# Diagonal weight tiles of a depthwise convolution, built during an earlier layer and kept in DRAM, loaded by DMA where they are used

## The chip, the cores and the metric

One core of a Trainium2 chip runs the whole program. The metric is the device time of one execution in microseconds (us); the median of three runs stands for a kernel.

The engines are named as the profile names them: PE is TensorE (matmuls; PEld are its weight loads), DVE is VectorE, ACT is ScalarE, POOL is GpSimd, and SP is the engine whose queue issues most of the DMAs here.

## The reference

A trunk of four layers on 512 tokens of width 1024. Layer 0 and layer 3 mix tokens by sliding-window attention, layer 1 by a conformer convolution module, layer 2 by a gated linear recurrence; every layer then has an MLP with squared ReLU and an inner width of 4096. All of it is float32. The part that matters here is the convolution module:

```
def conformer_conv(h, w_pw1, b_pw1, w_dw, b_dw, ln_g, ln_b, w_pw2, b_pw2):
    u = h @ w_pw1 + b_pw1
    a, gate = jnp.split(u, 2, axis=-1)
    u = a * jax.nn.sigmoid(gate)
    up = jnp.pad(u, ((0, 0), (CONV_WIDTH - 1, 0), (0, 0)))
    c = lax.conv_general_dilated(up, w_dw[:, None, :].astype(up.dtype), window_strides=(1,), padding='VALID',
                                 dimension_numbers=('NWC', 'WIO', 'NWC'), feature_group_count=D_MODEL)
    c = c + b_dw
    c = jax.nn.silu(layer_norm(c, ln_g, ln_b))
    return c @ w_pw2 + b_pw2

def squared_relu_mlp(h, w1, w2):
    return jnp.square(jax.nn.relu(h @ w1)) @ w2
```

`CONV_WIDTH` is 31, and each of the 1024 channels has its own 31 weights.

## The kernel before

**Matmuls and weights.** Every large matmul is done in float32 by three products of split operands (`step`, lines 285 to 287): high by high, high by low, low by high. A weight piece of 512 KB is loaded by a DMA on SP's queue into a tile `raw` (`fetch`, lines 245 and 251; `get`, line 212, for the MLP's second matrix), ScalarE casts it to `wh`, and VectorE makes `wl` = raw - wh (both line 262). There are three `raw` buffers for the first kind, eight for the second, and five pairs `wh`, `wl`. SP issues in the order in which the DMAs stand in its queue: one that waits for a buffer holds those behind it. GpSimd adds further pieces to a `raw` by accumulating DMAs on its own queue (line 217).

**The MLP** (`mlp`) runs four groups of 1024 inner columns. A group is a `linear` of 64 steps, whose eight PSUM tiles ScalarE squares into `us`, and then seven products of 56 steps in all, a fast 2 by 2 scheme. The products read operands `uh`, `ul` that VectorE and ScalarE make from `us` and its sums (lines 541 to 556), and VectorE adds each product into the rows (line 595).

**The convolution module** (`conformer`) runs a `linear` over eight channel blocks of 128. A block has two PSUM tiles, gate and `a`. `glu` takes each from PSUM on VectorE (line 921), ScalarE makes the sigmoid of the gate (line 924), and VectorE multiplies (line 930). Blocks 0 to 2 are then convolved on VectorE by 30 multiply-adds each over the row (line 884, "taps"). Blocks 3 to 7 are convolved on TensorE (`on_pe`): sixteen small ScalarE copies rearrange the block into `u` (line 903), four groups of nine matmuls each multiply it with a block-diagonal weight tile (line 824; the trace shows each as two), and sixteen small ScalarE copies bring the result out of PSUM (line 910). VectorE adds bias and shift (line 913; line 895 for the blocks of its own taps). Sums of the block and of its square are collected for the layer norm (`sums`, lines 849 to 861), and ones-matmuls turn them into means (`token_means`, line 401). When the last block is done, mean and scale are spread by TensorE (line 391), each block is centred, scaled and activated (lines 955 to 969), and the second projection begins.

**The weight tiles.** `Convolution` keeps them. A tile `w` is 128 x 34 x 32 floats, 557 KB; there are 20, four for each of the five blocks. `prepare` copies the 31 weights of the channels to a zeroed tile `taps` (line 802, sixteen copies of 32 partitions), and `build` multiplies `taps` with a 32 x 32 identity pattern `i4` on VectorE (line 814). Ten are built ahead, into ten buffers; each group used makes room for the next.

**What sets the order.** Work beside the matmuls is written as generators (`spawn`); each matmul step resumes them (`pump`), and `yield n` lets n steps pass. That gives the program's order, and a scheduler then fixes the order of each engine's own instructions. VectorE's taps are spaced by `PACE` steps. Each engine runs its instructions strictly in order.

## Time and profile before

| | us |
|---|---|
| median of three runs (2174.43 to 2178.05) | 2176.84 |
| profiled execution | 2178.24 |
| span of its trace | 2176.2 |
| PE busy | 2126.1 (98%) |
| DVE busy | 1417.7 (65%) |
| ACT busy | 1155.8 (53%) |
| POOL busy | 200.5 (9%) |

The profiled execution is 1.4 us above the median, and its trace covers all but 2.0 us of it. The first MLP lies at about 165 to 500 us of the span, the convolution module at about 500 to 730.

A row of a timeline gives the start and the duration in us, the engine, the line, the operation, its output and inputs, the shapes and how many instructions the row stands for; in brackets how long the engine stood idle before it, and what released it. Busy time of PE hides short waits between its matmuls, because their ends are modelled.

### The profile page before, as it was taken

The numbers are of one execution on the slowest core, as the hardware profiler recorded it, in microseconds if no ns is written. First come the engines' busy times: TensorE is split into PE (matmuls) and PEld (weight loads), VectorE is DVE, ScalarE is ACT, GpSimd is POOL, SyncE is SP. The second block draws the span as 40 slices with busy tenths as digits, with TensorE's granted clock in tenths as the row PEclk, the third lists the DMA queues.
The fourth block names the chain that finished last, engine by engine and source line by source line (L and its number), as shares of the span: only waits on it lengthen the run. The fifth ranks groups of instructions, "written<-read, shape, count | busy, mean of one in ns | idle before, by whom it ended". The sixth has DMA issues, their size and how long they took to land.

```text
span 2176.2 us, 27268 instructions
## 1 busy us (share of the span) xinstructions
PE 2126.1 (98%) x10226; PEld 1745.1 (80%) x10226; DVE 1417.7 (65%) x2250; ACT 1155.8 (53%) x2015; POOL 200.5 (9%) x193
## 2 busy tenths in 40 slices
PE   8999999999988999999999999999999999999997
PEld 7778788888877888888788888887888878888886
DVE  6864664759985375475888874547558784547547
ACT  6855454454684445445555554544546684534545
POOL 0000110110020011011300000101100000101100
PEclk9999999999998999999999999999999999999999
DMA  4154756745214375664322225567564116567553
GB/s 150 49 153 111 182 126 154 184 68 136 69 39 136 97 169 122 166 172 92 89 63 78 78 69 174 116 165 164 119 170 87 61 47 196 114 157 174 120 132 77
DMA packets 211063, 262.56 MB, mean 121 GB/s; under 512 B 9027, under 2 KB 136003, under 8 KB 210932
## 3 DMA queue, kind: packets, MB, share of 16 engines
q1 hardware_dynamic: 175540, 191.61, 27.7%
q0 software_dynamic: 35392, 69.21, 20.2%
q8 instruction: 81, 1.33, 0.3%
q14 instruction: 50, 0.41, 0.1%
HBM read 258.69 MB, written 2.10 MB: 120 GB/s over the span
## 4 chain that ended last, share of the span: by engine, by line
PE 71%; DVE 17%; ACT 4%; DMA 4%; issue 3%; SPq 0%; DVEq 0%; ACTq 0%
PE mm L287 20%; PE mm L286 20%; PE mm L285 20%; DVE wl L262 7%; DMA raw<-in_mlp_w_dram 4%; DVE rows L595 3%; DVE ul L556 2%; PE aux L745 2%; ACT wh L262 1%; PE aux L695 1%; PE aux L1059 1%; PE aux L438 1%; PE aux L824 1%; ACT uc L903 1%; DVE us_sum L547 1%
## 5 line engine op out<-in xcount | busy, mean ns | idle before, releaser
L262 DVE TENSOR_TENSOR wl<-raw,wh 128x1024 fp32r<-128x1024 f32 x452 | 550.9, 1221 | 528.4 <-ACT wh L262 525.1
L262 ACT CAST wh<-raw 128x1024 fp32r<-128x1024 f32 x452 | 467.9, 1047 | 492.5 <-DMA raw<-in_mlp_w_dram 206.1
L285 PE MATMUL mm<-x,wh 128*128 128x512 f32 x1568 | 629.9, 402 | 0.0
L287 PE MATMUL mm<-x,wl 128*128 128x512 f32 x1568 | 614.5, 392 | 7.6 <-DVE wl L262 7.6
L286 PE MATMUL mm<-x,wh 128*128 128x512 f32 x1568 | 613.3, 391 | 0.0
L287 PEld LDWEIGHTS mm<-x,wl 128*128 128x128 f32 x1568 | 294.5, 188 | 73.9 <-DVE wl L262 11.3
L285 PEld LDWEIGHTS mm<-x,wh 128*128 128x128 f32 x1568 | 295.3, 188 | 58.4 <-DVE rows L595 3.7
L286 PEld LDWEIGHTS mm<-x,wh 128*128 128x128 f32 x1568 | 295.3, 188 | 56.7 <-issue 1.8
L217 POOL DMA_DIRECT2D raw<-in_mlp_w_dram x128 | 153.5, 1206 | 1779.7 <-DVE wl L262 974.9
L285 PE MATMUL mm<-wh,uh 128*128 128x512 f32 x768 | 302.5, 394 | 7.1 <-DVE rows L595 4.4
L286 PE MATMUL mm<-wl,uh 128*128 128x512 f32 x768 | 299.2, 390 | 0.0
L287 PE MATMUL mm<-wh,ul 128*128 128x512 f32 x768 | 297.5, 390 | 0.2 <-DVE ul L556 0.2
L285 PEld LDWEIGHTS mm<-wh,uh 128*128 128x128 f32 x768 | 144.1, 188 | 45.7 <-DVE rows L595 8.1
L287 PEld LDWEIGHTS mm<-wh,ul 128*128 128x128 f32 x768 | 144.1, 188 | 31.2 <-DVE ul L556 0.6
L286 PEld LDWEIGHTS mm<-wl,uh 128*128 128x128 f32 x768 | 144.2, 188 | 28.2
L561 ACT ACTIVATE relu<-mm 128x512 f32<-128x512 f32 x128 | 75.9, 593 | 159.1 <-PE mm L287 159.1
L556 DVE TENSOR_TENSOR ul<-us,uh 128x1024 fp32r<-128x1024 f32 x64 | 78.0, 1219 | 32.5 <-ACT uh L555 32.5
L595 DVE SCALAR_TENSOR_TENSOR rows<-mm,nr,rows 128x512 f32<-128x512 f32 x128 | 95.1, 743 | 0.0
L562 ACT ACTIVATE us<-relu 128x512 f32<-128x512 f32 x128 | 81.0, 632 | 4.0
L285 PE MATMUL mm<-wh,y 128*128 128x512 f32 x192 | 78.0, 406 | 1.4 <-ACT y L366 1.4
L426 ACT ACTIVATE sq<-rows 128x512 f32<-128x512 f32 x64 | 40.2, 628 | 68.6 <-DVE rows L338 54.3
L287 PE MATMUL mm<-wh,y 128*128 128x512 f32 x192 | 76.0, 398 | 0.0
(232 smaller groups left out, 2564.8 us busy)
## 6 DMA issues: line engine op xcount, KB each, us to landing
raw<-in_mlp_w_dram SPq DMA_DIRECT2D x256, 512.0 KB
raw<-in_mlp_w_dram POOLq DMA_DIRECT2D x128, 512.0 KB, 6.1
raw<-in_hgrn_w_qfig_dram SPq DMA_DIRECT2D x64, 256.0 KB
raw<-in_attn_w_qkv_dram SPq DMA_DIRECT2D x20, 512.0 KB
raw<-in_attn_w_o_dram SPq DMA_DIRECT2D x16, 512.0 KB
raw<-in_conv_w_pw_dram SPq DMA_DIRECT2D x32, 256.0 KB
raw<-in_conv_w_pw_dram SPq DMA_DIRECT2D x8, 512.0 KB
raw<-in_hgrn_w_o_dram SPq DMA_DIRECT2D x8, 512.0 KB
```

The source lines that it names most:

```text
L217: gp.dma_start(out=wide(to), in_=block(w, r, c, h), accum_op=ALU.add)
L262: return sc.copy(wh, raw), ve.tensor_tensor(wl, raw, wh.bitcast(F32), ALU.subtract)
L285: pe.matmul(ps, sh, mh, start=start, stop=False, skip_group_check=again)
L286: pe.matmul(ps, sh, ml, start=False, stop=False, skip_group_check=again)
L287: pe.matmul(ps, sl, mh, start=False, stop=stop, skip_group_check=again)
L426: sc.activation(scratch("sq"), rows[:, b, f * T : (f + 1) * T], AF.Square, accum_out=self.ms[:, f, b : b + 1])
L438: pe.transpose(ps[:, b * P : (b + 1) * P], rows[:, b, j * P : (j + 1) * P], ident)
L556: ve.tensor_tensor(flat[1], src, flat[0].bitcast(F32), ALU.subtract)
L561: sc.activation(s, ps, AF.Relu)
L562: sc.activation(us[j // KH][:, :, j % KH, :], s.rearrange("p (h t) -> p h t", h=2), AF.Square)
L595: ve.scalar_tensor_tensor(o, banks[bank][p], norm.r2[sign][:, b : b + 1], o, ALU.mult, ALU.add)
L745: pe.matmul(po[h * HD : (h + 1) * HD, n * P : (n + 1) * P], vtok[:, n - 1 + b, kv * HD : (kv + 1) * HD], pT[:, b, n - n0, h, :], start=b = ...
```

## The change

The 20 weight tiles are no longer built in the convolution module. `prepare` takes a pool of the MLP of layer 0 and runs there as a task beside it: 40 half tiles of 128 x 17 x 32 floats are built on VectorE (line 809) in one buffer, and each is stored by a DMA on SP's queue to a tile in DRAM (line 812). In the convolution module `build` loads a whole tile by a DMA on SP's queue (line 832). Three things go with it: `PACE` falls from 2.4 to 1.8 steps per tap; the two accumulators of the layer norm get tiles of their own; and for the last block, 7, every second small copy, before and after its matmuls, goes to VectorE (line 920).

```diff
-PACE = 2.4
+PACE = 1.8
...
+            if beside:
+                spawn(beside(mp))
...
         def __init__(self):
...
+            dram = ctx.enter_context(tc.tile_pool(name="dram", bufs=1, space=bass.MemoryType.DRAM))
+            self.stored = [dram.tile([P, self.TAPS, 32], F32, name=f"w{n}") for n in range(4 * CONV_ON_PE)]
+            self.taps = const.tile([P, CONV_ON_PE, 4, self.TAPS], F32, name="taps")
...
+        def prepare(self, pool):
+
+            yield 24
             j0, r0 = KC - CONV_ON_PE, vrows["w_dw"]
...
+            nx = self.TAPS // 2
+            for n, stored in enumerate(self.stored):
+                for x in (0, nx):
+                    w = pool.tile([P, nx, 32], F32, tag="w", name="w")
+                    taps = self.taps[:, n // 4, n % 4, x : x + nx]
+                    ve.tensor_tensor(
+                        w, self.i4.unsqueeze(1).broadcast_to([P, nx, 32]), taps.unsqueeze(2).broadcast_to([P, nx, 32]), ALU.mult
+                    )
+                    nc.sync.dma_start(out=stored[:, x : x + nx, :], in_=w)
+                    yield 9
...
+        def ahead(self):
             for _ in range(self.AHEAD):
+                yield 4
                 self.build()
-                yield 3
...
-            ve.tensor_tensor(
-                w, self.i4.unsqueeze(1).broadcast_to([P, nx, 32]), self.taps[:, n // 4, n % 4, :].unsqueeze(2).broadcast_to([P, nx, 32]), ALU.mult
-            )
+            w = self.cp.tile([P, self.TAPS, 32], F32, tag="w", name="w", bufs=self.AHEAD)
+            nc.sync.dma_start(out=w, in_=self.stored[n])
...
-                    shared[k] = tmp.tile([P, T], F32, tag="acc", name=k, bufs=2)
+                    shared[k] = cp.tile([P, T], F32, name=k)
...
+            ends = j == KC - 1
+
+            def copy(o, src, r):
+                (ve.tensor_copy if ends and r % 2 else sc.copy)(o, src)
...
-                    sc.copy(cs[j][32 * g : 32 * g + 32, r::4], ps[32 * r : 32 * r + 32, :])
+                    copy(cs[j][32 * g : 32 * g + 32, r::4], ps[32 * r : 32 * r + 32, :], r)
...
-        mlp(i, mid, norm)
+        mlp(i, mid, norm, conv.prepare if i == 0 else None)
```

The order of the instructions moves at three places that matter.

VectorE in the linear of the first MLP's group 1, before, from the last product added into the rows (L595) to the sum of the first halves (L541):

```order
L595 SCALAR_TENSOR_TENSOR rows<-mm,r_1893,rows 128x512
L262 TENSOR_TENSOR wl<-raw,wh 128x1024 x5
L556 TENSOR_TENSOR ul<-us,uh 128x1024
L262 TENSOR_TENSOR wl<-raw,wh 128x1024 x4
L556 TENSOR_TENSOR ul<-us,uh 128x1024
L541 TENSOR_TENSOR us_sum<-us 128x1024
```

and in the change, from the same place on (L597 is the former L595, L558 the former L556):

```order
L597 SCALAR_TENSOR_TENSOR rows<-mm,r_1917,rows 128x512
L262 TENSOR_TENSOR wl<-raw,wh 128x1024
L809 TENSOR_TENSOR w<-i_145,taps 128x544 x2
L262 TENSOR_TENSOR wl<-raw,wh 128x1024
L809 TENSOR_TENSOR w<-i_145,taps 128x544
L262 TENSOR_TENSOR wl<-raw,wh 128x1024
L809 TENSOR_TENSOR w<-i_145,taps 128x544 x2
L262 TENSOR_TENSOR wl<-raw,wh 128x1024
L809 TENSOR_TENSOR w<-i_145,taps 128x544
L262 TENSOR_TENSOR wl<-raw,wh 128x1024
L558 TENSOR_TENSOR ul<-us,uh 128x1024
L809 TENSOR_TENSOR w<-i_145,taps 128x544 x2
```

One or two builds now stand before each cast. Of the 40 builds seven stand in the attention's projection, twelve in group 0's linear, thirteen in group 1's (one of them ahead of the row shown first, four behind the row shown last, before the second ul) and eight in group 2's; none stands among the products.

SP's queue at the same place, before, with the raw loads of the linear (L251) and of the products (L212):

```order
L251 DMA raw<-in_mlp_w_dram 128x4x256 x7
L212 DMA raw<-in_mlp_w_dram 128x2x512 x8
L251 DMA raw<-in_mlp_w_dram 128x4x256 x8
L212 DMA raw<-in_mlp_w_dram 128x2x512 x8
L251 DMA raw<-in_mlp_w_dram 128x4x256 x8
```

and in the change, from the products' loads of group 0 on:

```order
L212 DMA raw<-in_mlp_w_dram 128x2x512 x6
L251 DMA raw<-in_mlp_w_dram 128x4x256 x3
L812 DMA w_133<-w 128x544
L251 DMA raw<-in_mlp_w_dram 128x4x256 x2
L812 DMA w_134<-w 128x544 x2
L251 DMA raw<-in_mlp_w_dram 128x4x256
L812 DMA w_135<-w 128x544
L251 DMA raw<-in_mlp_w_dram 128x4x256
L812 DMA w_135<-w 128x544
L812 DMA w_136<-w 128x544
L251 DMA raw<-in_mlp_w_dram 128x4x256
L812 DMA w_136<-w 128x544
```

The stores (`w_133` and so on are the tiles in DRAM) stand among the raw loads, the first of the group behind three of them.

VectorE at the end of the convolution's linear, before, from the end of block 1's taps:

```order
L884 SCALAR_TENSOR_TENSOR uc<-uc,vecT 128x493
L895 TENSOR_TENSOR uc<-uc,shift 128x512
L913 SCALAR_TENSOR_TENSOR uc<-uc,vecT,shift 128x512
L262 TENSOR_TENSOR wl<-raw,wh 128x1024
L921 TENSOR_TENSOR a<-mm,r_4308 128x512
L884 SCALAR_TENSOR_TENSOR uc<-uc,vecT 128x494
L930 SCALAR_TENSOR_TENSOR a<-a,vecT,gate 128x512
L884 SCALAR_TENSOR_TENSOR uc<-uc,vecT 128x495
```

and in the change (L900, L911, L934, L942 and L951 are the former L884, L895, L913, L921 and L930):

```order
L900 SCALAR_TENSOR_TENSOR uc<-uc,vecT 128x511
L911 TENSOR_TENSOR uc<-uc,shift 128x512
L942 TENSOR_TENSOR a<-mm,r_4474 128x512
L262 TENSOR_TENSOR wl<-raw,wh 128x1024
L934 SCALAR_TENSOR_TENSOR uc<-uc,vecT,shift 128x512
L942 TENSOR_TENSOR a<-mm,r_4474 128x512
L951 SCALAR_TENSOR_TENSOR a<-a,vecT,gate 128x512
L262 TENSOR_TENSOR wl<-raw,wh 128x1024
L920 COPY uc<-a 32x128 x8
L934 SCALAR_TENSOR_TENSOR uc<-uc,vecT,shift 128x512
L875 TENSOR_TENSOR acc_4832<-acc_4832,uc 128x512
L876 TENSOR_TENSOR acc_4833<-acc_4833,csq 128x512
```

All taps, block 2's too, now stand ahead of block 7's two tiles; behind them come VectorE's share of the small copies of block 7 and the sums of block 6.

## Rows read from the trace of the kernel before

**Rows 1.** Page, part 1: engine, busy us (share of the span) x instructions
```profile
PE 2126.1 (98%) x10226; PEld 1745.1 (80%) x10226; DVE 1417.7 (65%) x2250; ACT 1155.8 (53%) x2015; POOL 200.5 (9%) x193
```

**Rows 2.** Windows: us; busy of PE, PEld, DVE, ACT, POOL; granted clock; DMA share; GB/s
```profile
520.00:540.00 20.00, 20.00 (x90) 16.57 (x89) 20.00 (x26) 7.59 (x9) 0.00 (x0) 1.00 0.50 132
560.00:580.00 20.00, 19.25 (x114) 15.65 (x113) 16.25 (x22) 16.63 (x37) 0.00 (x0) 1.00 0.15 53
660.00:665.00 5.00, 4.62 (x22) 4.47 (x21) 0.17 (x1) 0.00 (x0) 0.00 (x0) 0.50 1.04 387
```

**Rows 3.** Timeline of PE after the linear: start us, us, instruction, count [idle before <-releaser]
```profile
622.77 9.48 PE L824 MATMUL aux<-uc,w 128*128 128x128 f32 x72
...
641.26 11.75 PE L824 MATMUL aux<-uc,w 128*128 128x128 f32 x72 [9.01 <-ACT uc L910]
...
657.53 3.55 PE L401 MATMUL aux<-ones_d,acc 128*128 128x1 f32 x16 [4.52 <-ACT csq L854]
...
663.12 1.84 PE L401 MATMUL aux<-ones_d,csq 128*128 128x1 f32 x8
...
670.59 0.80 PE L285 MATMUL mm<-wh,z 128*128 128x512 f32 x1 [1.58 <-ACT z L366]
```

**Rows 4.** Timeline of DVE at the end of the convolution
```profile
627.95 0.75 DVE L913 SCALAR_TENSOR_TENSOR uc<-uc,vecT,shift 128x512 f32<-128x512 f32 x1 [3.40 <-ACT uc L910]
...
629.75 0.68 DVE L921 TENSOR_TENSOR a<-mm,r 128x512 f32<-128x512 f32 x1
...
631.41 1.75 DVE L930 SCALAR_TENSOR_TENSOR a<-a,vecT,gate 128x512 f32<-128x512 f32 x1
...
646.60 8.79 DVE L884 SCALAR_TENSOR_TENSOR uc<-uc,vecT 128x503 f32<-128x503 f32 x9
```

**Rows 5.** Timeline of ACT at the end of the convolution
```profile
611.37 6.96 ACT L903 COPY uc<-a 32x128 f32<-32x128 f32 x16 [4.52 <-DVE a L930]
...
633.19 6.83 ACT L903 COPY uc<-a 32x128 f32<-32x128 f32 x16 [2.49 <-DVE a L930]
...
640.03 5.87 ACT L910 COPY uc<-aux 32x128 f32<-32x128 f32 x15
```

**Rows 6.** The lines L814 and L802: duration ns min/median/max, first and last start
```profile
L814 DVE TENSOR_TENSOR w<-i,taps x20: 1277/1281/1294, 515.9 to 616.2; 128x1088 f32<-128x1088 f32 x20
...
L802 DVE COPY taps<-vecT x16: 236/249/329, 508.0 to 515.6; 32x155 f32<-32x155 f32 x16
```

**Rows 7.** Timeline of DVE in the first MLP, groups 0 and 1
```profile
171.15 1.41 DVE L447 SCALAR_TENSOR_TENSOR x<-aux,vecT,x 128x512 fp32r<-128x512 f32 x2
...
212.93 1.23 DVE L262 TENSOR_TENSOR wl<-raw,wh 128x1024 fp32r<-128x1024 f32 x1 [1.49 <-ACT wh L262]
...
293.74 1.23 DVE L262 TENSOR_TENSOR wl<-raw,wh 128x1024 fp32r<-128x1024 f32 x1 [6.93 <-ACT wh L262]
...
296.46 1.23 DVE L262 TENSOR_TENSOR wl<-raw,wh 128x1024 fp32r<-128x1024 f32 x1 [1.49 <-ACT wh L262]
...
298.71 1.23 DVE L556 TENSOR_TENSOR ul<-us,uh 128x1024 fp32r<-128x1024 f32 x1 [1.02 <-ACT uh L555]
```

**Rows 8.** Timeline of ACT at the start of group 1
```profile
252.78 1.05 ACT L262 CAST wh<-raw 128x1024 fp32r<-128x1024 f32 x1 [6.17 <-DMA raw<-in_mlp_w_dram]
...
262.30 1.05 ACT L262 CAST wh<-raw 128x1024 fp32r<-128x1024 f32 x1 [0.53 <-DMA raw<-in_mlp_w_dram]
```

**Rows 9.** Timeline of SP at the start of group 1
```profile
246.94 3.96 SPq L251 DMA_DIRECT2D raw<-in_mlp_w_dram  x3
```

**Rows 10.** Timeline of SP, the last output store
```profile
2172.69 0.33 SPq L511 DMA_DIRECT2D out_dram<-rows  x1
```

**Rows 11.** Waits of SP: line waited for, us in total, times, longest
```profile
SPq L1261 <- DMA out_dram<-rows: 1.7, 1, 1.7
```

**Rows 12.** Page, part 6: DMA issues, count, KB each, median us to landing
```profile
raw<-in_mlp_w_dram POOLq DMA_DIRECT2D x128, 512.0 KB, 6.1
```

**Rows 13.** Windows, raw loads of the first MLP
```profile
166.00:175.00 9.00, 9.00 (x49) 7.46 (x49) 6.33 (x12) 6.52 (x11) 0.00 (x0) 1.00 0.77 235
```

31 lines of the change are left out of this document (14 added, 17 removed).

## The prediction

> **What bounds the kernel now.** The page's first part comes first: TensorE is busy for 98% of the span [rows 1], so an edit elsewhere pays only where TensorE stands still. The windows by stretch show where that is. In the convolution's linear (520 to 580) TensorE is nearly always busy, 19.25 of 20 us at the worst; behind it, at 660 to 665, it runs at half the granted clock, 0.50 [rows 2]. The timeline of TensorE shows the stretch between [rows 3]: the linear ends at 622.8; block 6's 72 convolution matmuls follow; then TensorE is idle for 9.01 us until ScalarE's PSUM copies (L910) free it, and for 4.52 us before the means (L401); the first projection matmul comes at 670.59, some 48 us after the linear.
>
> Why the two waits are there is read from VectorE and ScalarE. Block 7's last tile is ready at 622.9, but VectorE takes it (L921) at 629.75, because L913 of block 5, which stands before it in VectorE's order, waited 3.40 us for ScalarE's L910; L930 then lasts until 633.16 [rows 4]. ScalarE waits for L930 twice: 4.52 us at block 6 and 2.49 us at block 7. Its sixteen copies of block 7 (0.43 us each) run from 633.19 to 640.03, and the PSUM copies of block 6, which hold the banks block 7 needs, stand behind them [rows 5]. So VectorE, loaded with taps and weight tiles, is the first cause; ScalarE's chain of small copies passes it on; and nine taps left over hold VectorE from 646.60 to 655.39, ahead of block 7's last shift [rows 4].
>
> **The change part by part.**
>
> *Taken out of the convolution's VectorE.* Twenty builds at a pitch of about 1.21 us (1.28 us each, overlapping) are 24.2 us, and sixteen tap copies at 0.26 are 4.2 us [rows 6]: 28 us. The faster pace puts some 20 taps (about 0.66 us each) ahead of the last tile that ran behind it before: 13 us back. VectorE gains about 15 us before 623 and keeps up. Block 6's gated tile, late by at least the 4.52 us that ScalarE waited, moves up, ScalarE's queue with it, and L934 of block 5 (L913 before) no longer holds block 7's last tile.
>
> *The tail, step by step.* Last tile from PSUM at 623.2, gated (0.6 + 0.74) at 624.5. ScalarE, after its casts and squares, starts its eight copies at about 625.6 and ends at 629.0; VectorE's eight, at 0.25 us by the nearest row [rows 6], end sooner. Block 6's PSUM copies follow at 629.0 and free the first bank by 630.6. TensorE ends block 6 at 632.0 and goes on to block 7 there, not at 641.26. Its 72 matmuls take 9.4 us, and about 2 us of waiting for the partial sums (L875, L876), whose means now stand among them: end near 643.5. Four last PSUM copies, ScalarE and VectorE in turn, 1.4 us, shift 0.75, square 0.63: 646.5. Of the 32 ones matmuls 16 are left (1.84 us for eight at half clock [rows 3]): 650. From there as now (664.96 to 670.59, 5.63 us) to the first projection matmul at about 655. Gain 15.5 us: 13 if something slips by a PSUM copy or two, 19 if the clock stays at full speed.
>
> *Less waiting for VectorE in the linear.* The 0.75 us missing at 560 to 580 [rows 2] goes: 0.8 us.
>
> *The loads.* Twenty of 557 KB, 11.1 MB on SP's queue. At the 235 GB/s that loads reach in the first MLP [rows 13] each takes 2.4 us, 47 us in all, in a stretch where the engines are half busy at first and 0.15 later [rows 2]. Tiles lie ten ahead, so I take 0; without that cover the price is what a late raw load costs, up to 2 us.
>
> *The builds in the first MLP.* Forty at half size, 0.64 us each by the row of the full ones: 26 us. All stand in the linear phases or in the attention's projection, where VectorE idles up to 6.93 us at a time [rows 7]; none stands among the products. Their work is covered. What is not is the single buffer: a build waits until the store before it has landed, and the casts queued behind it on VectorE wait too, as do the raw loads behind a store on SP.
>
> *What a store's flight is.* The trace has no such store. The nearest row is the last output store, same queue and direction, twice the size: 0.33 us of issue and a wait of 1.7 us [rows 10, 11] give at least 2.0, and by the span's end at most 3.5. The far end is an accumulating load, 6.1 us [rows 12]. I take 2.6, and 1.1 more (half a raw load of 512 KB at 235 GB/s) when a raw load is just ahead. Spacing of two builds: 0.64 + 2.6 = 3.2 us plain, 4.3 behind a raw load.
>
> *Group 0.* Twelve builds, five of them behind raw loads: 7 x 3.2 + 5 x 4.3 = 44 us, against 41.8 us from the x rows at 171.15 to the cast at 212.93 [rows 7]. Part of the raw loads is ahead by then, and the products' first operands have slack: 1.5 us, with the projection's seven builds. *Group 1* is worse, because it begins in a backlog. Three raw loads are issued from 246.94 [rows 9]; ScalarE gets the first at 252.78 and the third at 262.30 [rows 8], 12 us after issue. The phase's first store stands behind them and cannot land before about 263.5. Eleven spacings of about 3.6 us follow: the last build ends near 304, where now the last cast runs at 296.46 and the operand ul at 298.71 [rows 7]. That operand would be 7 us late; the second product needs it about 1.5 us after it is ready now: TensorE loses about 6 us. *Group 2* has eight builds, which end near 287 by the same count, with time to catch up: 0. Cost 7.5 us. The ends: with landings of 2.0 us group 1's last build ends by 293, cost 0.5; with 6.1 us everywhere, 12 x 6.7 - 42 = 39, 263.5 + 74 - 296 = 41, and some 8, near 90 us. The output store is nearer than an accumulation, so the range takes spacings of up to 4.3 us: 12 x 4.3 - 41.8 = 10 and 263.5 + 11 x 4.3 + 0.6 - 296.5 = 15, 25 us.
>
> By the Trainium skill, DMA: Bandwidth & Descriptors, section "Latency and other measured facts", memory latency is 0.2 us on average but 2 us at high load, and it makes most of a transfer's fixed cost. By that rule a store among raw loads would land some 1.8 us later than one in the quiet end of the kernel, whose row I used; the spacing would be about 5 us, an estimate, the two groups would cost 41 us, and the sum would be 2202 us. No row here shows a store under load.
>
> **The sum.** The profiled execution took 2178.24 us. 2178.24 - 15.5 - 0.8 + 7.5 = 2169.4; it stands 1.4 us above the median of the runs, so 2168 us. A measurement of this kernel can tell about 0.2%, 4.4 us: "same" is 2172.5 to 2181.2.
>
> **The rivals.**
> *The stores pace the first MLP (slower).* One mechanism: VectorE waits for a landing before each build, and the lateness reaches the products' operands. It decides from a mean spacing of about 4.2 us, where groups 0 and 1 cost 9 and 14 us, more than the gain, and the time passes 2181; at 4.5 they cost 12 and 17, and the time is 2178.2 - 16.3 + 29 - 1.4 = 2190. For it: loads in group 1 do take 6 to 12 us [rows 8, 9], and the operand is on the path. Against: only the first store of that phase stands behind three loads, the later ones behind one or none. The page's rule above is this case with a price. Chance 0.16.
> *The tail stays bound by small copies.* ScalarE's PSUM copies and the alternation of two engines on one bank could keep half of the waits, and the edit on VectorE would matter little: gain 8 instead of 15.5, 2175.5. For it: the 9.01 us name ScalarE, not VectorE. Against: ScalarE itself waits for L930 [rows 5]. Chance 0.13.
> *Better than forecast.* Stores land in 2.0 us, cost 0.5, and the clock, which fell after TensorE had stood idle, stays up, gain 19: 2178.2 - 19.8 + 0.5 - 1.4 = 2157.5. Chance 0.16.
> The forecast itself, 2160 to 2175, has 0.55.
>
> **How the numbers follow.** The range takes the best case's 2155 at one end and, at the other, spacings of up to 4.3 us, 2178.2 - 16.3 + 24 - 1.4 = 2184; beyond lies the rest of the slower rival. Faster by over 0.2%: the best case, nine tenths of the forecast and a little of the copies' rival, 0.68; slower 0.16; same 0.16.
>
> **What would show it.** Right: in the changed profile block 7's 72 matmuls start within 1 us of block 6's end; L951 of block 7 ends before 626; the first projection matmul comes about 48 - 15 = 33 us after the linear; in group 1's linear VectorE idles before L809 for landings, ul comes some 7 us later against the phase's start, and group 0 loses under 3 us. Wrong: idle time before L809 adding up to far more than 3 us a build, or TensorE waiting for ul or wl by over 15 us in the first MLP; a wait of over 3 us between blocks 6 and 7; new waits for raw loads in the convolution's linear.

## The result, and the profile after

| | us |
|---|---|
| before, median of six runs on this chip (2174.43 to 2178.28) | 2177.69 |
| changed kernel, median of six runs (2186.02 to 2194.43) | 2190.31 |
| ratio, with its 95% interval | 1.0059 (1.0049 to 1.0070) |
| changed kernel, profiled execution | 2188.81 |
| span of its trace | 2187.1 |

The change makes the kernel slower by 0.6%. The forecast was 2168 us with a range of 2155 to 2184, faster with 0.68: wrong in sign, and 2190 lies outside the range.

Three marks split the time in every trace. **A** is the first transpose of the rows behind the first MLP (L438), **B** the first of block 6's 72 convolution matmuls, where the linear of the convolution module ends, **C** the first projection matmul. Before they stand at 493.75, 622.77 and 670.59 us. The timeline of TensorE in the changed kernel:

```profile
506.98 0.27 PE L438 MATMUL aux<-ident,rows 128*128 128x128 f32 x1
...
578.18 1.81 PE L884 MATMUL aux<-uc,ones 128*128 128x512 f32 x2 [4.52 <-DVE uc L900]
...
641.48 9.48 PE L840 MATMUL aux<-uc,w 128*128 128x128 f32 x72
652.46 5.17 PE L840 MATMUL aux<-uc,w 128*128 128x128 f32 x24 [1.50 <-ACT uc L920]
658.84 1.02 PE L401 MATMUL aux<-ones_d,acc 128*128 128x1 f32 x8 [1.20 <-DVE acc L875]
...
661.30 8.74 PE L840 MATMUL aux<-uc,w 128*128 128x125 f32 x46
672.61 1.02 PE L401 MATMUL aux<-ones_d,uc 128*128 128x1 f32 x8 [2.58 <-DVE uc L934]
...
680.52 0.80 PE L285 MATMUL mm<-wh,z 128*128 128x512 f32 x1 [1.58 <-ACT z L366]
```

A stands 13.2 us later than before: that is the price of what now stands ahead of it, the tap copies, the builds and the stores (e1 below has the copies alone and loses 0.8 us). From A to B the linear takes 134.5 us (129.0 before): it became 5.5 us longer. From B to C it is 39.0 us against 47.8: here are the gains, 8.8 us of the 15.5 forecast. Of the waits of [rows 3] the 9.01 us between blocks 6 and 7 are down to 1.50, and in place of the 4.52 us before the means there are 1.20 before the partial sums and 2.58 before the last means. But a new wait of 4.52 us stands in the middle of the linear, before L884, the ones matmul that takes the shift from block 0; it waits for L900, block 0's last tap on VectorE. Behind that wait the granted clock is 0.50 from 578.43 to 581.84, so the linear loses more than the wait itself. In all 13.2 + 5.5 - 8.8 = 9.9 us at C, and 10.6 at the end of the profiled execution.

The windows of the changed kernel, beside [rows 2] (us; busy of PE, PEld, DVE, ACT, POOL; granted clock; DMA share; GB/s):

```profile
560.00:580.00 20.00, 15.48 (x64) 11.82 (x63) 17.42 (x24) 11.91 (x22) 0.00 (x0) 0.96 0.30 91
620.00:640.00 20.00, 20.00 (x120) 16.90 (x119) 16.99 (x20) 15.89 (x34) 4.63 (x3) 1.00 0.37 133
640.00:660.00 20.00, 17.30 (x114) 14.88 (x113) 12.78 (x17) 17.00 (x41) 6.35 (x4) 0.91 0.17 53
660.00:680.00 20.00, 16.10 (x88) 14.76 (x86) 7.25 (x22) 5.47 (x12) 0.00 (x0) 0.68 0.43 160
```

The hole in the linear is the first row, 15.48 of 20 us. In the last row the granted clock is 0.68 in the mean, so part of it at 1.2 GHz in place of 2.4, over the 46 matmuls of block 7 and the means: TensorE had stood still three times behind B, for 1.50, 1.20 and 2.58 us. The page's first part hardly shows any of it; it stands against [rows 1]:

```profile
PE 2132.3 (97%) x10226; PEld 1746.5 (80%) x10226; DVE 1427.9 (65%) x2286; ACT 1149.4 (53%) x1999; POOL 199.2 (9%) x193
```

VectorE at the end of the convolution, beside [rows 4]:

```profile
576.15 1.23 DVE L262 TENSOR_TENSOR wl<-raw,wh 128x1024 fp32r<-128x1024 f32 x1 [2.35 <-ACT wh L262]
577.29 0.74 DVE L900 SCALAR_TENSOR_TENSOR uc<-uc,vecT 128x511 f32<-128x511 f32 x1
...
626.21 1.75 DVE L951 SCALAR_TENSOR_TENSOR a<-a,vecT,gate 128x512 f32<-128x512 f32 x1
...
643.01 1.23 DVE L262 TENSOR_TENSOR wl<-raw,wh 128x1024 fp32r<-128x1024 f32 x1 [5.67 <-ACT wh L262]
...
645.28 0.68 DVE L942 TENSOR_TENSOR a<-mm,r 128x512 f32<-128x512 f32 x1
646.00 1.33 DVE L951 SCALAR_TENSOR_TENSOR a<-a,vecT,gate 128x512 f32<-128x512 f32 x1
...
649.58 4.27 DVE L920 COPY uc<-a 32x128 f32<-32x128 f32 x8
```

Block 7's tile leaves PSUM (L942) at 645.28 and is gated from 646.00 on, 4.5 us behind B. The wait that was L913's [rows 4] has moved to the cast ahead of it: wl waits 5.67 us for ScalarE's wh, which stands behind ScalarE's copies of block 6. The tap that L884 needs, at 577.29, stands behind such a cast too.

VectorE in the first MLP, beside [rows 7]: first the group of the 40 builds (busy, mean ns of one, idle time before them), then the timeline of group 1.

```profile
L809 DVE TENSOR_TENSOR w<-i,taps 128x544 f32<-128x544 f32 x40 | 29.0, 725 | 71.6 <-DMA w<-w 70.3 <-PE aux L747 1.2
```

```profile
177.29 0.73 DVE L809 TENSOR_TENSOR w<-i,taps 128x544 f32<-128x544 f32 x1 [1.63 <-DMA w<-w]
...
268.63 0.72 DVE L809 TENSOR_TENSOR w<-i,taps 128x544 f32<-128x544 f32 x1 [3.71 <-DMA w<-w]
...
288.05 0.72 DVE L809 TENSOR_TENSOR w<-i,taps 128x544 f32<-128x544 f32 x1 [0.59 <-DMA w<-w]
293.42 0.72 DVE L809 TENSOR_TENSOR w<-i,taps 128x544 f32<-128x544 f32 x1 [4.64 <-DMA w<-w]
294.06 1.22 DVE L262 TENSOR_TENSOR wl<-raw,wh 128x1024 fp32r<-128x1024 f32 x1
296.29 0.72 DVE L809 TENSOR_TENSOR w<-i,taps 128x544 f32<-128x544 f32 x1 [1.01 <-DMA w<-w]
...
302.62 0.72 DVE L809 TENSOR_TENSOR w<-i,taps 128x544 f32<-128x544 f32 x1 [4.47 <-DMA w<-w]
...
310.17 1.22 DVE L558 TENSOR_TENSOR ul<-us,uh 128x1024 fp32r<-128x1024 f32 x1
```

and the matmul that reads the operand in the last row:

```profile
311.45 0.50 PE L287 MATMUL aux<-wh,ul 128*128 128x512 f32 x1 [4.00 <-DVE ul L558]
```

VectorE stands idle 70.3 us before the builds, 1.8 us for each, until the store before has landed. Group 1's operand ul comes at 310.17 (298.71 before), and the second product waits 4.00 us for it at 311.45. TensorE runs the same matmuls up to A in both kernels, in the same order but for a stretch of the attention (44 to 138 us), so from there on the start of each matmul can be set against that of the same matmul before: it is 2.0 us later at the end of the attention's products, 4.8 in the first steps of the MLP, 6.0 at the start of group 1, 11.9 behind its second product, 13.2 at A.

### The profile page after: what moved, and what is told of

It is laid out like the page before. It is cut to its first block, busy times and chain, and to the rows that moved or that the text cites. A ratio compares the mean times of both kernels' runs of the same rounds, so it can differ in the third digit from the quotient of the medians.

```text
span 2187.1 us, 27431 instructions
## 1 busy us (share of the span) xinstructions
PE 2132.3 (97%) x10226; PEld 1746.5 (80%) x10226; DVE 1427.9 (65%) x2286; ACT 1149.4 (53%) x1999; POOL 199.2 (9%) x193
## 4 chain that ended last, share of the span: by engine, by line
PE 59%; DVE 18%; DMA 10%; issue 7%; ACT 5%; SPq 0%; POOL 0%; DVEq 0%; ACTq 0%; POOLq 0%
PE mm L287 17%; PE mm L286 17%; PE mm L285 17%; DVE wl L262 7%; DMA raw<-in_mlp_w_dram 5%; DMA w<-w 4%; DVE rows L597 4%; DVE ul L558 2%; ACT wh L262 2%; PE aux L747 2%; PE aux L697 1%; PE aux L1080 1%; ACT uc L920 1%; PE aux L840 1%; DVE us_sum L543 1%
## 5 line engine op out<-in xcount | busy, mean ns | idle before, releaser
L558 DVE TENSOR_TENSOR ul<-us,uh 128x1024 fp32r<-128x1024 f32 x64 | 78.1, 1220 | 28.5 <-ACT uh L557 28.5
L597 DVE SCALAR_TENSOR_TENSOR rows<-mm,nr,rows 128x512 f32<-128x512 f32 x128 | 95.3, 744 | 0.0
L285 PE MATMUL mm<-wh,y 128*128 128x512 f32 x192 | 78.2, 407 | 1.4 <-ACT y L366 1.4
L557 ACT CAST uh<-us_sum 128x1024 fp32r<-128x1024 f32 x48 | 50.6, 1055 | 51.9 <-DVE us_sum L543 30.6
```

What stands on the lines that cost most here:

```text
L285: pe.matmul(ps, sh, mh, start=start, stop=False, skip_group_check=again)
L557: sc.copy(flat[0], src)
L558: ve.tensor_tensor(flat[1], src, flat[0].bitcast(F32), ALU.subtract)
L597: ve.scalar_tensor_tensor(o, banks[bank][p], norm.r2[sign][:, b : b + 1], o, ALU.mult, ALU.add)
```

## The experiments

Fifteen kernels, each a few lines away from the change or from the kernel before. First their marks, read as above from the timeline of TensorE in each trace. The change run again (e5) has 506.79, 640.38 and 680.89, within 1.1 us of the first trace at B and 0.4 at A and C. The spread between kernels is wider: up to A the change, e2, e4, e5 and e13 run the same instructions in the same order on every engine, and A lies at 506.8 to 510.5; e4, e6 and e7 have the same order on TensorE, VectorE, ScalarE and GpSimd from A to C, and take 34.5 to 36.8 us from B to C. So a difference of 2 us between two traces says little. A ratio is to the kernel before on the same chip, whose median is 2175.5 to 2177.7.

| | A | A to B | B to C | median | ratio to before (95%) |
|---|---|---|---|---|---|
| before | 493.75 | 129.0 | 47.8 | 2177.69 | |
| the change | 506.98 | 134.5 | 39.0 | 2190.31 | 1.0059 (1.0049 to 1.0070) |
| e1 convolution's part, pace 1.8 | 494.54 | 136.9 | 39.1 | 2171.62 | 0.9981 (0.9972 to 0.9991) |
| e2 MLP's part | 510.53 | 128.2 | 42.6 | 2187.91 | 1.0050 (1.0033 to 1.0067) |
| e3 two buffers | 505.21 | 135.2 | 38.4 | 2186.54 | 1.0047 (1.0032 to 1.0062) |
| e4 the change, pace 2.4 | 506.91 | 128.1 | 34.5 | 2182.77 | 1.0024 (1.0014 to 1.0034) |
| e5 the change again | 506.79 | 133.6 | 40.5 | 2187.83 | 1.0053 (1.0038 to 1.0068) |
| e6 convolution's part, pace 2.4 | 494.12 | 128.2 | 36.1 | 2163.23 | 0.9943 (0.9928 to 0.9958) |
| e7 builds pinned | 499.60 | 128.6 | 36.8 | 2173.79 | 0.9988 (0.9979 to 0.9998) |
| e8 12 of 20 tiles stored | 493.78 | 128.0 | 37.2 | 2162.23 | 0.9937 (0.9922 to 0.9951) |
| e9 before, pace 1.8 | 493.04 | 131.5 | 55.6 | 2185.52 | 1.0043 (1.0028 to 1.0058) |
| e10 stores, no builds | 497.27 | 128.2 | 42.6 | 2176.66 | 1.0007 (0.9997 to 1.0016) |
| e11 builds, no stores | 494.50 | 128.2 | 42.2 | 2166.89 | 0.9959 (0.9945 to 0.9973) |
| e12 e6 without halved copies | 494.44 | 128.2 | 38.8 | 2165.70 | 0.9954 (0.9939 to 0.9969) |
| e13 the change, shift later | 509.12 | 128.9 | 41.0 | 2185.78 | 1.0045 (1.0030 to 1.0060) |
| e14 tap copies ahead, nothing stored | 495.53 | 128.2 | 41.6 | 2167.25 | 0.9961 (0.9946 to 0.9976) |
| e15 e8 with pace 2.8 | 492.84 | 128.0 | 35.0 | 2159.23 | 0.9921 (0.9904 to 0.9938) |

Of the medians, those of e2, e6, e10, e12 and e14 lie in the band that was written down for the theory, e1, e4, e8 and e11 below it; e3, e7, e9, e13 and e15 fell between the two bands, and e5 just below its second.

Behind C all kernels run the same code. The span from C to the trace's end is 1500.5 to 1507.0 us, 1505.6 before; this part of the differences is taken up at the end.

**e1, e2: the two halves of the change.** e1 leaves out the builds and stores; the loads stay and read a slice of an MLP weight. e2 keeps the builds and stores, and lets the convolution build its tiles on VectorE at pace 2.4, with all small copies on ScalarE.

e1:

```diff
-            for n, stored in enumerate(self.stored):
+            for n, stored in enumerate(self.stored[:0]):
...
-            nc.sync.dma_start(out=w, in_=self.stored[n])
+            nc.sync.dma_start(out=w.rearrange("p x c -> p (x c)"), in_=mlp_w1[0][:P, : 32 * self.TAPS])
```

e2:

```diff
-PACE = 1.8
+PACE = 2.4
...
-            nc.sync.dma_start(out=w, in_=self.stored[n])
+            nx = self.TAPS
+            ve.tensor_tensor(
+                w, self.i4.unsqueeze(1).broadcast_to([P, nx, 32]), self.taps[:, n // 4, n % 4, :].unsqueeze(2).broadcast_to([P, nx, 32]), ALU.mult
+            )
...
-            ends = j == KC - 1
+            ends = False
```

> The changed kernel without the 40 builds and stores in the first MLP; the twenty loads of the convolution stay, of the same size and shape, but read a piece of the first MLP's matrix, so the convolution of blocks 3 to 7 has other weights. In the changed kernel the convolution's linear begins 13.2 us later in the span than before (508.18 against 494.95, first matmul behind the spread). Theory A, the store's round trip in the single buffer makes all of these 13 us: time about 2177 (2175 to 2179), the convolution's linear begins at 495 to 497. Rival, the lateness comes from the sixteen tap copies in the attention and from SP's order of loads, which both stay or change little: time above 2184.

> The changed kernel with the convolution as before: full tiles built on VectorE, no loads, pace 2.4, all small copies on ScalarE; the builds and stores of the first MLP stay and nobody reads them. Theory A: the first MLP costs 13 us as in the changed kernel, and the convolution gives nothing back but the tap copies that it no longer does: 2187 to 2191. Rival, the loads in the convolution are what is slow: 2177 to 2181.

e1: 2171.62 us, hardly faster than before, though the first MLP costs it nothing: A is 0.8 us later, and the convolution gains 0.8 (176.1 from A to C against 176.8). e2: 2187.91 us; A is 16.8 us later. So neither half does what the forecast said: the convolution's part gives back in the linear (+7.9) what it gains behind it (-8.7), and the MLP's part costs over twice the 7.5 us. In e1 L884 waits as in the change:

```profile
567.96 2.04 PE L884 MATMUL aux<-uc,ones 128*128 128x512 f32 x2 [4.97 <-DVE uc L900]
```

e2 shows one thing more: its convolution, which builds on VectorE like the kernel before, is 6.1 us shorter (170.8). What it does not do there any more is copy the taps.

**e3: a second buffer for the builds** (room for it made by one scratch tile less).

```diff
-    tmp = ctx.enter_context(tc.tile_pool(name="tmp", bufs=6))
+    tmp = ctx.enter_context(tc.tile_pool(name="tmp", bufs=5))
...
-                    w = pool.tile([P, nx, 32], F32, tag="w", name="w")
+                    w = pool.tile([P, nx, 32], F32, tag="w", name="w", bufs=2)
```

> The changed kernel with two buffers for the built halves in the first MLP instead of one (one scratch buffer of 2 KB fewer makes room). Theory A, the wait for a landing before each build is the cost: idle time before the builds falls from 70 us to under 25, group 1's second product no longer waits (4.17 us before), the first MLP costs 3 to 6 us instead of 13, time 2180 to 2184. Rival B, the raw loads and the stores hold each other up on SP's queue, whatever the buffers: within 3 us of the changed kernel, 2187 to 2193.

2186.54 us. VectorE's idle time before the builds falls from 70.3 to 33.4 us, but A comes only 1.8 us earlier. The builds had moved: with a buffer free the scheduler puts them further ahead on VectorE, 34 of the 40 before 225 us, so the attention's projection and group 0 now pay what group 1 paid (the same matmul is 4.3 us late at the MLP's first steps, 10.1 at group 1's start). A wait that is halved is not a cost that is halved when the order is free to move. What the missing scratch tile costs by itself was not tried.

**e10, e11: stores without builds, builds without stores.** Both start from e2.

e10:

```diff
-                    w = pool.tile([P, nx, 32], F32, tag="w", name="w")
-                    taps = self.taps[:, n // 4, n % 4, x : x + nx]
-                    ve.tensor_tensor(
-                        w, self.i4.unsqueeze(1).broadcast_to([P, nx, 32]), taps.unsqueeze(2).broadcast_to([P, nx, 32]), ALU.mult
-                    )
-                    nc.sync.dma_start(out=stored[:, x : x + nx, :], in_=w)
+                    w = self.taps.rearrange("p j g x -> p (j g x)")[:, : nx * 32]
+                    nc.sync.dma_start(out=stored[:, x : x + nx, :].rearrange("p x c -> p (x c)"), in_=w)
```

e11:

```diff
-                    nc.sync.dma_start(out=stored[:, x : x + nx, :], in_=w)
```

> As the second run (the convolution as before, its builds on VectorE, pace 2.4), but in the first MLP the 40 builds are left out and the 40 stores, of the same size and at the same places of the program, write other data straight from the taps; nothing reads them. So SP's queue and the DMA traffic stay, VectorE has no build and no wait for a landing. Theory (VectorE's wait for each landing is the cost): first projection matmul at 671 to 674 us (670.6 before, 681.3 with builds and stores), median 2176 to 2180. Rival (stores among the raw loads make these late): 679 us or more, median 2185 to 2188.

> As the second run, but the 40 stores are left out: 40 builds of half a tile in the first MLP, into one buffer, with nothing to wait for; the tiles built there are not read. Theory (the wait for landings is the cost, the builds themselves stand beside other work): first projection matmul at 670.6 to 673 us, median 2175 to 2179. Rival (the 29 us of VectorE's own work, and the tap copies in the attention, are the cost): 677 us or more, median 2183 to 2188.

A stands at 497.27 and 494.50: 3.5 and 0.8 us for stores alone and builds alone, 16.8 for both (e2). So at least 12 us of e2's cost are the link between the two, VectorE's wait for a landing with the casts queued behind it, and neither the traffic nor VectorE's 29 us of work. In e11 the group of the builds reads:

```profile
L809 DVE TENSOR_TENSOR w<-i,taps 128x544 f32<-128x544 f32 x40 | 28.9, 722 | 2.1 <-PE aux L747 1.2
```

Both first projection matmuls, 668.05 and 664.93, lie below the bands that were written down, which counted the convolution as before: it is 6.1 and 6.4 us shorter again (170.8 and 170.4). e11, which does nothing useful in the first MLP, is 0.4% faster than the kernel before.

**e4, e6, e9: the pace.** e4 is the change with pace 2.4, e6 is e1 with it, e9 the kernel before with 1.8; one line each.

e4 and e6:

```diff
-PACE = 1.8
+PACE = 2.4
```

e9:

```diff
-PACE = 2.4
+PACE = 1.8
```

> The changed kernel with the old pace of the taps, 2.4 steps each. In the changed kernel TensorE waits 4.52 us at 573 for block 0's last tap on VectorE. Theory C, the faster pace puts block 0's ones-matmul ahead of what VectorE can do: the wait goes, 4 to 5 us in the linear, of which the tail takes some back since more taps stand behind the last tile: 2185 to 2188. Rival D, VectorE is late there because the first ten loads of weight tiles hold up the raw loads behind them on SP's queue: the wait stays at 3 us or more, 2188 to 2192.

> The convolution's part alone (no builds, no stores, loads of other data as in the first experiment), with the old pace of 2.4 steps per tap. Theory C, the faster pace spoils the convolution: the linear's wait for block 0's last tap goes and the tail shortens as it did with builds and stores at this pace (162.7 us from the first matmul of the linear to the first projection matmul, 175.6 before): 2161 to 2166. Rival, the pace only mattered behind a late first MLP: 2169 to 2173.

> The kernel before with one number changed: PACE 1.8 in place of 2.4. Theory (the faster pace costs by itself: taps put ahead on VectorE delay the casts of the linear and block 7's two tiles): the convolution lasts longer by at least the 11 to 12 us that the pace cost in the two pairs of runs without builds there, since here VectorE has the 28 us of builds besides; from the convolution's first matmul to the first projection matmul 187 us or more (175.6 before), median 2187 to 2200. Rival (the pace only fills VectorE's room where there is some, and the cost came from the loads that stand among the raw loads): with the builds on VectorE and no loads, the pace costs under 4 us, median 2176 to 2180.

The pace alone makes the kernel before slower by 9.8 us (2185.52 against 2175.67) and e6 slower by 8.4 (2171.62 against 2163.23). By the marks, A to C, it costs 10.2 us from before to e9, 11.8 from e6 to e1 and 10.9 from e4 to the change. With the builds in the first MLP the medians show less: 5.1 us from e4 to e5, 7.5 to the change's first median. And they show more for the builds and stores, which stand at 13 us by A: 18.7 us from e1 to the change, 19.5 from e6 to e4. In part that is the choice of the execution that was profiled: e4's (2176.78) is the fastest of ten that reach 2184.45, e1's (2176.05) the slowest of ten that begin at 2170.06. Why these scatter stays open. With pace 2.4 no wait stands before L884, and the tail comes near what was forecast:

```profile
635.04 9.48 PE L840 MATMUL aux<-uc,w 128*128 128x128 f32 x72
645.54 9.58 PE L840 MATMUL aux<-uc,w 128*128 128x128 f32 x72 [1.03 <-ACT uc L920]
...
669.58 0.50 PE L285 MATMUL mm<-wh,z 128*128 128x512 f32 x1 [1.58 <-ACT z L366]
```

Block 7's 72 matmuls follow block 6's after 1.03 us and run in one piece; A to B is 128.1, B to C 34.5. In e9, TensorE:

```profile
568.35 1.55 PE L868 MATMUL aux<-uc,ones 128*128 128x512 f32 x2 [1.87 <-DVE uc L884]
...
624.58 9.47 PE L824 MATMUL aux<-uc,w 128*128 128x128 f32 x72
...
657.50 1.83 PE L401 MATMUL aux<-ones_d,acc 128*128 128x1 f32 x8 [10.15 <-DVE acc L859]
...
680.13 0.50 PE L285 MATMUL mm<-wh,z 128*128 128x512 f32 x1 [1.58 <-ACT z L366]
```

Here the ones matmul waits 1.87 us, and the partial sums 10.15 us in the middle of block 7's matmuls, for sums that VectorE adds only after the nine taps that it had left. The faster pace did not make VectorE faster: it put the matmuls that use its results earlier into TensorE's order. Nor is it the pace that moves the taps ahead of block 7's last tile: behind that tile VectorE still has 18 taps to do before, 16 in e9, 13 in e11 and e14, whose tap copies are gone from the module, and none in e4 and in the change, whose builds are gone as well.

**e13: the ones matmul later.** The change, pace 1.8; L884 moves on TensorE behind 42 of block 3's 72 convolution matmuls (none of them ahead of it in the change, 54 in e4).

```diff
         def first_shift():
 
-            yield 4
+            yield 16
```

> The change with one number altered: `first_shift` lets 16 steps pass in place of 4 ahead of the ones matmul that reads block 0 (L884), which puts that matmul behind block 3's 72 convolution matmuls on TensorE, where it stood ahead of the linear's next step. Pace 1.8 stays. Theory (the faster pace costs because it puts this matmul into TensorE's order before VectorE has finished block 0's taps): the wait of 4.52 us before L884 and the clock's fall behind it go; from the first transpose behind the first MLP to the first projection matmul 165 to 169 us (173.5 in the change), median 2180 to 2185. Rival (VectorE is behind by that much in any case, and the same time is lost at the next place that needs it): 172 us or more, median 2186 to 2190.

A to C is 169.9 us, between the two bands (173.5 in the change). TensorE:

```profile
586.00 1.02 PE L884 MATMUL aux<-uc,ones 128*128 128x512 f32 x2
...
638.03 9.48 PE L840 MATMUL aux<-uc,w 128*128 128x128 f32 x72
651.75 6.01 PE L840 MATMUL aux<-uc,w 128*128 128x128 f32 x24 [4.24 <-ACT uc L920]
```

The wait is gone and with it the whole loss in the linear: A to B is 128.9, as before. But only 3.6 us of the 5.6 arrive at C. Block 7 starts 13.7 us behind block 6 (11.0 in the change, 10.5 in e4, 12.0 in e6), because VectorE reaches block 6's tile (L951) at 625.50, 12.5 us ahead of B, where e4 reaches it at 618.95, 16.1 us ahead, and ScalarE's copies, its cast and block 7's tile follow in a chain. The same 141 instructions of VectorE stand ahead of that tile from A on in both kernels; in e13 it idles 14.2 us among them (11.5 in e4; what is more are waits for ScalarE's casts), and the 81 taps among them take 62.7 us (60.0). From block 7's first matmul to C it is 27.3 us, against 24.0 in e4. The partial sums still split block 7's matmuls, but wait only 0.37 us; most of the difference lies ahead of them. While TensorE stands still for 4.24 us the granted clock falls (us; busy of PE, PEld, DVE, ACT, POOL; granted clock; DMA share; GB/s):

```profile
650.28:657.10 6.82, 5.35 (x22) 4.57 (x22) 3.43 (x8) 5.91 (x16) 1.05 (x1) 0.50 0.21 74
```

The first 24 matmuls take 6.01 us, where all 72 take 9.58 in e4, so 2.8 us are lost in them. Of the pace's 10.9 us by the marks a third, then, is the place of one matmul; 3.2 are VectorE's lateness at block 6's tile, 2.8 the lower clock behind the wait that this makes, and 1.2 are left. With traces that differ by 1 to 2 us these are sizes and no more. The median, 2185.78, is 2 us below e5, with A 2.3 us later.

**e12, e14: the small parts.** e12 is e6 with all of block 7's copies on ScalarE. e14 stores and loads nothing and builds in the convolution as before, but keeps the tap copies ahead of the module, the accumulators' own tiles and the halved copies.

e12:

```diff
-            ends = j == KC - 1
+            ends = False
```

e14:

```diff
-PACE = 1.8
+PACE = 2.4
...
-            for n, stored in enumerate(self.stored):
+            for n, stored in enumerate(self.stored[:0]):
...
-            nc.sync.dma_start(out=w, in_=self.stored[n])
+            nx = self.TAPS
+            ve.tensor_tensor(
+                w, self.i4.unsqueeze(1).broadcast_to([P, nx, 32]), self.taps[:, n // 4, n % 4, :].unsqueeze(2).broadcast_to([P, nx, 32]), ALU.mult
+            )
```

> As the sixth run (tiles loaded, no builds or stores in the first MLP, pace 2.4; the loads read a slice of an MLP weight, so the convolution is computed with other weights), but all 32 small copies of block 7 stay on ScalarE. Theory (VectorE's load was the first cause of the two waits at the end of the convolution, the halved copies add a few us): 3.4 us for eight copies ahead of block 7's matmuls, up to 1.5 more behind them; first projection matmul at 661 to 664 us (658.4 with halves), median 2165 to 2169. Rival (the small copies bind the tail): most of the 12.2 us goes, first projection matmul at 667 to 671, median 2172 to 2176.

> No weight tile is stored or loaded: the convolution module builds its 20 tiles on VectorE as the kernel before does, at pace 2.4. Of the change there stay the sixteen tap copies ahead of the module, the accumulators' own tiles and block 7's halved copies. Theory (the terms add: 6.1 to 6.4 us from the first two, as in the three runs that had them with the builds in the convolution, and 2.8 from the halved copies): first transpose to first projection matmul 167 to 169 us (176.8 before), nothing lost in the first MLP, median 2166 to 2169. Rival (what the second, tenth and eleventh runs gained in the convolution came with their stores or builds in the first MLP): 173 us or more, median 2172 to 2177.

e12: 38.8 us from B to C against 36.1, so the halved copies give 2.7 us, as expected; its wait between blocks 6 and 7 is 6.32 us. e14: A to C 169.8 us, 7.0 less than before, and a median of 2167.25. That is a little worse than the band for A to C (167 to 169): with the builds on VectorE the halved copies give only 0.6 to 1.0 us (e10 and e11, without them, have 170.8 and 170.4). The terms do not quite add, but the sizes are plain: the 4.2 us of tap copies, taken out of the start of the module, are worth about 6 us there (e2, e10, e11), at a price of 0.8 to 1.8 us at A (e11, e14), and the 24 us of builds only 3 to 6 more (e12 against e11, e6 against e14). VectorE in e11 shows how, beside [rows 4] and [rows 6]:

```profile
499.57 1.28 DVE L832 TENSOR_TENSOR w<-i,taps 128x1088 f32<-128x1088 f32 x1
...
645.92 4.88 DVE L902 SCALAR_TENSOR_TENSOR uc<-uc,vecT 128x508 f32<-128x508 f32 x4
```

The first build starts at 499.57, not at 515.9, behind sixteen copies; VectorE is busy in that stretch in both kernels. At the end four taps are left ahead of block 7's sums, in 4.88 us, not nine in 8.79. The accumulators' own tiles came with the copies in all these runs and were not taken apart from them.

**e7, e8, e15: versions.** e7 is the change with pace 2.4 and the builds kept in the program's order, one every six steps and, but for the first, only in the linears of the four groups (`phase` says when one runs); the tap copies come sooner, too. e8 builds the first eight tiles on VectorE in the convolution and stores only the last twelve, 24 half builds, nine steps apart. e15 is e8 with pace 2.8.

e7 (e8 has `[8:]`, `yield 9`, and builds the first eight tiles as the kernel before does):

```diff
-PACE = 1.8
+PACE = 2.4
...
-            yield 24
+            yield 1
...
-                yield 6
+                yield 1
...
-            for n, stored in enumerate(self.stored):
+            for n, stored in list(enumerate(self.stored))[0:]:
...
-                    ve.tensor_tensor(
+                    while not phase["linear"]:
+                        yield 1
+                    keep(ve.tensor_tensor(
...
-                    yield 9
+                    yield 6
```

> The changed kernel at pace 2.4, its builds held where the program emits them: ten or eleven in each of the four linear phases, every six steps (4.1 us), one in the projection and none pulled ahead by the scheduler. Theory A, a build costs only where less than a store's round trip (some 3.5 us) lies between two of them: the first MLP costs 2 to 6 us instead of 12, time 2164 to 2171. Rival B, what costs is the stores' traffic and place on SP's queue, which stays: 2176 to 2183.

> As the one before, but the first eight tiles are built on VectorE at the start of the convolution, where it idles until block 0 is gated (12.3 of 20 us busy at 520 to 540 of the changed kernel), and only twelve go through DRAM: 24 builds in the first MLP, every nine steps, seven or eight in a linear phase. Theory A: the first MLP costs 0 to 3 us and the convolution keeps its gain of 13: 2163 to 2168, the fastest of all. If the eight builds delay the taps, the wait for block 0's last tap comes back: 2168 to 2173.

> The eighth run's kernel with pace 2.8 in place of 2.4. Theory (taps too early hurt the linear, taps too late hold block 7's sums at the end, and 2.4 lies near the best): within 3 us of the eighth run, median 2160 to 2166. Rival (VectorE's taps are in the way of the linear at 2.4 too): the linear ends earlier by some us more, median 2155 to 2159.

e7: 2173.79 us; A at 499.60, 5.9 us later than before, where the free order cost 13.2 (e4); order, spacing and start of the builds were altered together. e8: 2162.23 us; A at 493.78, where it is before: 24 builds with room between them cost nothing, though VectorE still idles before them for 23.7 us. e15: 2159.23 us, the best kernel here, 0.8% faster than before. Its 144 matmuls of blocks 6 and 7 run in one piece:

```profile
620.89 18.88 PE L851 MATMUL aux<-uc,w 128*128 128x128 f32 x144
```

The linear ends no earlier than in e8 (128.0 from A to B in both), and behind it 2.2 us are gained. The two kernels ran on different chips, and the intervals of their ratios overlap: that 2.8 is a better pace than 2.4 is not shown, only that a slower pace than the change's does no harm.

**e5: the change again**, beside e6 to e8, with no line altered.

> The changed kernel once more, unaltered, beside the other runs of this group on the same chip. If its parts add up, it takes what the two halves gave alone: 2176.0 - 4.4 (convolution alone) + 11.9 (first MLP alone) = 2183.5. If they work on each other (a later or differently loaded start of the convolution), it stays at 2188 to 2192 as measured first.

2187.83 us, 1.0053 of before: the result holds, and the parts do not add up (2183.5).

## Why the prediction was wrong

Two steps failed. With the old pace alone the change is still 0.2% slower than before (e4), without the builds and stores alone it is 0.2% faster (e1), and without them at the old pace 0.6% faster (e6). Between the forecast and the trace lie 18.7 us at C (-8.8 against +9.9). By the marks the pace has 10.9 of them, the builds 5.7, and the tail at the old pace 2.2; by the medians the builds weigh more than the pace.

**The pace, costed at nothing.** The step reads "The faster pace puts some 20 taps (about 0.66 us each) ahead of the last tile that ran behind it before: 13 us back. VectorE gains about 15 us before 623 and keeps up." It looked at VectorE's work alone, and the taps ahead of the last tile came with the builds' leaving, not with the pace (18 behind it before, 16 in e9, none in e4). What a pace also sets is where the matmuls that use the taps stand in TensorE's order: the ones matmul of block 0 and the partial sums. VectorE did not keep up with those places, and TensorE, which runs its matmuls in order, stood still for them: 4.52 us in the linear at 578.18, 1.20 us among block 7's matmuls at 658.84, in the timeline above, with 3.4 and 6.8 us at the lower granted clock (0.50) close behind. The Trainium skill, PSUM — Partial Sum Buffer, section "Engine vs sequencer instructions", says that matmuls start and complete in program order; the trace agrees, no matmul of the linear runs in those 4.52 us. With the rest of the change left as it is, the pace is worth 10.9 us by the marks and 5.1 to 7.5 by the medians (e4); in the kernel before it is 10.2 and 9.8 (e9).

**With the old pace the forecast of the convolution comes near.** The linear's 0.8 us: 0.9 measured in e4. The tail's 15.5 us, with 13 as its lower end: 13.3 in e4 (47.8 to 34.5), but 11.7 in e6 and 11.0 in e7, whose convolutions are the same but for what e6 loads. The loads' 0: ScalarE did wait for raw loads behind the tiles at the module's start, but A to B is the same 128.2 us with loads (e6, e12) as without (e10, e11). What carried the gain was put down wrongly in part: the builds got most of the credit (24.2 of 28 us), and e14 shows that the tap copies ahead, the accumulators' own tiles and the halved copies bring 7.0 us from A to C, half or more of it, without a tile in DRAM.

**The second term, mis-sized: the builds, 7.5 us.** Measured 13.2 at A, and 13.0 to 16.8 in the five traces with this order up to A; the kernels without this cost (e1, e6, e8, e9, e11, e12, e14, e15) have A between 0.9 us earlier and 1.8 later than before. Most of the surplus of e2 and e13 stands in the attention's projection, where one build waits 6.56 and 5.62 us for its landing (3.68 in the change). By the medians builds and stores cost 18.7 and 19.5 us (e1 to the change, e6 to e4); what lies behind A in that is not known. Group 1, forecast at 6 us, cost 5.9, and its operand came 5.5 us late against the phase's own start (11.5 less 6.0; forecast 7). The spacing of builds was 2.9 us in twelve places (293.42 to 296.29 is one), near the 3.2 forecast, and behind the first build of groups 0 and 1 it is 3.9 and 3.6 in the mean. The error is in the parts taken as nearly free: the attention's end, its projection and the MLP's start cost up to 4.8 us (a build at 177.29 stands before the x rows; 1.7 of the 4.8 are there in e11 without stores, too), group 0 another 1.2, the end of the MLP 1.3, instead of 1.5 and 0. A build that waits in the attention's projection delays the last sums of the rows (L338), which stand behind it on VectorE, and with them TensorE's transposes; that queue was not looked at.

**The rival that gave 2190 us was not what happened.** It wanted 29 us of cost in the first MLP from a mean spacing of 4.5 us, with the tail's full gain; the traces show 3.9 and 3.6, 13 us there, and the rest in the convolution. That its number fits is chance. The rival of the small copies (8 us instead of 15.5) names the measured gain, 8.8, but not its cause: at pace 2.4 the same copies let 11.0 to 13.3 through.

**The signs written down.** Block 7 starts 1.50 us behind block 6 (1 was the limit), its L951 ends at 647.3, not before 626 (639 with the 13 us of the MLP), and C comes 39.0 us behind the linear, not 33: all three say that VectorE was late. Idle time before L809 is 1.8 us a build, TensorE's wait for ul 4.0 us: no runaway there, as these lines say. The line that should have been in the list is a new wait in the linear for a result of VectorE. Two ends of the range do not meet their sums: the lower is called the best case's 2155, whose own sum is 2157.5, and the upper takes 24 us where the count gives 25. At 2190 neither matters.

## What to carry to other kernels

A pace, a lag or any number that spaces work in a program's order is a promise to the in-order engine that uses the results: before it is tightened, look up where its consumers then stand, and what stands behind them there. Where an edit takes work off an engine, try the cheap parts alone first (here e14, with sixteen small copies moved ahead, eight plus eight given to VectorE, two tiles of their own and no new traffic, gave 8 of the 16 us that the best kernel has). Where a build has to wait until the store before it frees the one buffer, every cast queued behind it waits for that landing, too; 24 builds spread over the steps that have room cost nothing at A (e8), 40 with a free order 13 to 17 us.

## What was not expected of the hardware

**Stores beside accumulating loads.** Build to build the spacing is 2.9 us at its least, but 5.4 us from 288.05 to 293.42 and 6.3 us from 296.29 to 302.62. Just ahead of both stands an accumulating load of GpSimd's queue:

```profile
286.63 1.19 POOL L217 DMA_DIRECT2D raw<-in_mlp_w_dram  x1 [29.45 <-DVE wl L262]
295.58 1.20 POOL L217 DMA_DIRECT2D raw<-in_mlp_w_dram  x1 [7.77 <-DVE wl L262]
```

A store that meets one lands some 2.5 to 3.5 us later. By the trace's DMA packets the stores issued at 288.8 and 297.0 move nothing until 291.9 and 300.7, about where the loads' packets end (292.1 and 301.3); two stores of group 0, issued at 200.2 and 208.2, wait for such loads in the same way. So the stores stand behind the loads; that they share engines is the likely reason, and was not tried by itself. The prediction set the rule of the Trainium skill, DMA: Bandwidth & Descriptors, section "Latency and other measured facts", against its own row: by an estimate from its figures a store under load should land about 1.8 us later, with a spacing of about 5 us. In size the trace agrees for the stores beside an accumulating load, whose delay is the wait just told; among plain raw loads the spacing in the linears is mostly 2.9 to 3.6 us, with 4.9 and 5.2 at 177.29 and 356.69.

**VectorE's copies beside GpSimd.** Eight copies of 32x128 take 4.27 us at 649.58 in the change and 2.28 us in e4, where GpSimd has nothing to do at that time; in the change GpSimd adds squares of the blocks then (L876, 648.43 to 652.01). The durations in ns (least, median, most) in the change and in e4:

```profile
L920 DVE COPY uc<-a x8: 261/268/1323, 649.6 to 653.6; 32x128 f32<-32x128 f32 x8
L920 DVE COPY uc<-a x8: 261/266/271, 642.7 to 644.7; 32x128 f32<-32x128 f32 x8
```

Two of the eight last 1.23 and 1.32 us, and each ends 0.13 us behind one of GpSimd's two additions; the other six are as short as in e4. The Trainium skill, SBUF — State Buffer, section "Who interferes with whom", tells that VectorE and GpSimd share a pair of ports, that a copy of VectorE can take it, and that the one which issues first holds it for its whole instruction while the other waits; the trace agrees with it. How much of it reached TensorE was not taken apart.

**Behind C.** The same code from C to the end of the trace took 1500.5 us (e11) to 1507.0 us (e7). The difference grows by about 0.3 us a group in the later MLPs, whose products VectorE paces, and its cause stays open. The eight kernels with 40 stores have 1504.6 us or more, those with 24 or none 1503.8 or less, but the kernel before, with none, has 1505.6. Some 4 us of the best kernels' gain lie there.
